# A decoder layer on one core: turnings grouped by bank, a tile in another pool, a scaling moved behind later splits

## The chip, the cores and the metric

The kernel runs on one core of a Trainium2 chip. The metric is the device time of one execution in microseconds (us). The kernel before takes 1844.71 us, the median of three runs (1843.94 to 1847.14).

## What is computed

One decoder layer on 256 tokens of width 2048, in float32:

```
x  = x + 0.5 * swiglu(rms_norm(x, ffn1_norm))             # D_FF = 5632
h  = rms_norm(x, mix_norm);  P = h @ w_in                  # columns split among head groups
     A: gated linear attention, 4 heads (dk 64, dv 128), output rms-normed per head and gated by silu(g_r)
     B: sparse attention, 8 query heads, 2 kv heads: compressed, selected and window branches
     C: cross-attention, 4 heads, into 256 memory tokens (memory normed, projected by w_mem_kv)
x  = x + concat(A, B, C) @ w_out
x  = x + 0.5 * swiglu(rms_norm(x, ffn2_norm))
y  = rms_norm(x, final_norm)
```

## The kernel before

**Products.** Every float32 product runs as three passes of TensorE. A chunk of weights, 128 x 1024 (512 KB), is loaded into a tile `r`; ScalarE copies it into a rounded tile `h` (L293), VectorE makes the remainder `l = r - h` (L294), and `mm3` (L313 to L316) issues left-high by `h`, left-low by `h` and left-high by `l`. In the trace these are the lines L314, L315 and L316, 128 x 512 each. `mmchunk` issues 12 of them for a chunk, and `product` eight chunks for a product. The left side of each product (`hh`/`hl`, `xh`/`xl`, `oh`/`ol`, `zh`/`zl`) is an activation that stands transposed in SBUF, also split in high and low.

**Stages.** `ffn1`, the mixing stage (projections "agq", "gkks", ..., "kwvs", "vw", the attention groups, then four products with `wout`) and `ffn2` follow each other. Each stage opens its own SBUF and PSUM pools (`stage`, L203) where the pools of the stage before lay, so a tile of a new stage may lie on bytes that an old tile held, and its first load then waits for the old tile's last reader.

**Turnings.** Between stages the residual `acc` is squared, turned by TensorE against an identity (`transposed`, L346, the turnings are L352), and split by ScalarE (L343) and VectorE (L344) with the gains of the next norm. One PSUM bank takes two blocks `k` of 128 columns, two turnings each. The last quarter of `acc` is turned inside the first product of the next stage (`turn_last`, L711).

**Norms.** `rstd` (L336) makes `(ss/n + eps)^-0.5` on GpSimd: a multiply-add (L338) and a power (L339). `headnorm` (L832) squares on VectorE (L834), sums (L835) and calls it.

**Order.** The program is written as one stream; a scheduler puts each engine's instructions into an order by the dependencies and the order of writing. `behind_products` (L297) pins what is written under it behind the latest split or product matmul of the engines named. `placed` calls a task ahead of a chunk of a product. All loads of weights go through SP's queue, in order, but for the adds of `ffn1u` and `ffn2u` from GpSimd, and for the first chunk of `ffn1g`, which ScalarE's queue issues.

**Around the change.** The gated output of group A stands in `ov` (L1040 to L1046): scaled by the head norm (L1045), multiplied by the gate (L1046), turned into `oh` by `turn_out` inside the projection "kwvs". The memory keys `mh` are scaled (L1218, L1219) and turned (L1226) inside the second memory product; the memory attention (scores L1259, softmax, turnings L1277, products L1289) is drained from there on. `gaT` is a small tile of the pool `own`, which lies below the pools `lo`, `raw` and `hi` of the mixing stage. Pool `ev` has two buffers of 128 x 512.

Of the kernel before, what the change touches and what calls it, by code (L numbers as in the profile page):

```python
# [22 lines left out]
D = 2048  # L23
# [168 lines left out]
def _body(tc, A):  # L192
# [24 lines left out]
    def bank():  # L217
        return psum("pm", "pm")
# [4 lines left out]
    def tbank():  # L223
        return psum("pt" if "pt" in P else "px", "pt")
# [76 lines left out]
            ex.enter_context(tc.issue_after(getattr(i, "ins", i)))  # L301
        return ex

    def chunk(src, parts=1, queue=nc.sync):
        n = src.shape[1]
        r = raw(n)
        for i in range(parts):
            sl = slice(i * n // parts, (i + 1) * n // parts)
            queue.dma_start(r[:, sl], src[:, sl])
        h, l = split(r, parts)  # L310
        return h.rearrange("p (k n) -> p k n", k=2), l.rearrange("p (k n) -> p k n", k=2)

# [10 lines left out]
            done["pe"] = mm3(banks[t][:, :n], ah[:, k0 + kk, sl], al[:, k0 + kk, sl], h[:, kk], l[:, kk],  # L323
                             first and kk == 0, last and kk == 1)

    def product(banks, ah, al, src, before=None, parts=1, queue=nc.sync):
        for c in range(8):
            if before:
                before(c)
            w = chunk(src[c], parts, queue) if c == 0 else chunk(src[c])  # L330
            mmchunk(banks, ah, al, 2 * c, w, c == 0, c == 7)

    def t16(name, dt=F32R):
# [1 line left out]

    def rstd(ss, inv_n, n, np_=128):  # L336
        y = small(n, "y")[:np_]
        pool.tensor_scalar(y, ss, inv_n, EPS, op0=ALU.mult, op1=ALU.add)  # L338
        pool.tensor_tensor(y, y, neghalf[:np_].to_broadcast([np_, n]), op=ALU.pow)  # L339
        return y  # L340

    def scaled_split(dh, dl, src, g):
        act.activation(dh, src, AF.Identity, scale=g)  # L343
        dve.scalar_tensor_tensor(dl, src, g, f(dh), op0=ALU.mult, op1=ALU.subtract)  # L344

    def transposed(j, g, th, tl, ks=range(4)):  # L346
        for k in ks:
            if k % 2 == 0:
                pt = (tbank() if "pt" in P else bank()).rearrange("p (k t) -> p k t", k=2)
            b = 4 * j + k  # L350
            for t in range(2):
                pe.transpose(pt[:, k % 2, t * 128:t * 128 + 128], acc[:, t, b * 128:b * 128 + 128], ident)  # L352
            scaled_split(th[:, b], tl[:, b], pt[:, k % 2], g[:, b:b + 1])

    def square_acc(ss, j):
        for t in range(2):
# [38 lines left out]
                 ("up", 5): lambda: put(3, 12, "tensor_add", 12, 22)}  # L395
        return (sh, sl), lambda *at: steps.get(at, lambda: None)()

    def ffn(name, th, tl, r, after, before=lambda i: None, by_rows=None, plain=(), queue=nc.sync):

# [23 lines left out]
        def first_slab():  # L425
            pg, pu = [bank(), bank()], [bank(), bank()]
            s4, made = combine(th, tl)

            def in_gate(c):
                before(c)  # L430
                made("gate", c)

            def in_up(c):
                made("up", c)
                before(("up", c))
                if c == 7:
                    for t in range(2):
                        st = t512("sil")
                        act.activation(st, pg[t], AF.Silu, scale=rr(t))
                        sil.append(st)  # L440

            sil, gs = [], []
            product(pg, th, tl, wg[0], in_gate, 2, queue)
            product(pu, th, tl, wu[0], in_up)
            for t in range(2):
                g = t512("g")
                dve.scalar_tensor_tensor(g, pu[t], rr(t), sil[t], op0=ALU.mult, op1=ALU.mult)
                gs.append(g)
            return s4, gs
# [144 lines left out]

    def load_x(c):
        r = t512("xT").rearrange("p (k t) -> p k t", k=2)
        nc.sync.dma_start(r, A["xT"][c])
        if c == 0:
            nc.sync.dma_start(gains, A["gains"])
        for k in range(2):  # L600
            b = 2 * c + k
            scaled_split(hh[:, b], hl[:, b], r[:, k], C["g1"][:, b:b + 1])
# [101 lines left out]
        elif at == (3, 10):  # L704
            norm_mem()

    ffn("ffn1", hh, hl, r1, after1, before1, queue=nc.scalar)
    xh, xl = st1["h"], st1["l"]
    r2, rm, r2q, r2n = (keep.tile([128, 2], F32, name=n) for n in ("r2", "rm", "r2q", "r2n"))

    def turn_last(c, ss, g, th, tl):  # L711

        if c == 1:

            for i in late_adds:
                tc.add_manual_dep(i.ins, done["dve"].ins.name, ORDER, reason="order")
        if c in (2, 3):
            with behind_products():
                transposed(3, g, th, tl, range(2 * c - 4, 2 * c - 2))
        if c == 4:  # L720
            with behind_products():
                square_acc(ss, 3)
# [72 lines left out]
    dve.tensor_scalar_add(gates, gates, 1.0)  # L795
    dve.reciprocal(gates, gates)

    gaT = own.tile([128, 256], F32, name="gaT")
    la = []

    def turn_ga():
# [227 lines left out]
        dve.tensor_tensor(sgr[:, t].rearrange("p (h d) -> p h d", h=4), xg.rearrange("p (h d) -> p h d", h=4),  # L1029
                          C["gon"].unsqueeze(1).to_broadcast([128, 4, 128]), op=ALU.mult)  # L1030

    ovs = []
    for t in range(2):
        pb = mbank()
        p3 = pb.rearrange("p (h d) -> p h d", h=4)
        for h in range(4):
            pe.matmul(p3[:, h], at[t][:, h], gv[:, t, h * 128:h * 128 + 128], start=True, stop=t == 0)
            if t == 1:
                pe.matmul(p3[:, h], at[2][:, h], gv[:, 0, h * 128:h * 128 + 128], start=False, stop=True)
        ov = t512("ov")  # L1040
        ovs.append(ov)
        act.activation(ov, pb, AF.Copy)
        rs = headnorm(ov, 4)
        o3 = ov.rearrange("p (h d) -> p h d", h=4)
        dve.tensor_tensor(o3, o3, rs.unsqueeze(2).to_broadcast([128, 4, 128]), op=ALU.mult)  # L1045
        dve.tensor_mul(ov, ov, sgr[:, t])  # L1046
    oh, ol = t16("oh"), t16("ol")

    def put_heads(src, k0, t):
# [11 lines left out]


    vsw = b4("vsw").rearrange("p (b c d) -> p b c d", b=2, c=2)
    b = proj("kwvs", both(spread("v", 0), placed((4, lambda: turn_out(0)), (5, lambda: turn_out(1)))))
    for t in range(2):
        s = r2[:, t:t + 1]
        v = ev("kw", 256)
# [167 lines left out]
    for i in range(2):  # L1235
        b = [bank(), bank()]
        for c in range(4):
            r = raw().rearrange("p (k t) -> p k t", k=4)
            nc.sync.dma_start(r, A["memT"][c])
            h = hi().rearrange("p (k t) -> p k t", k=4)  # L1240
            l = lo().rearrange("p (k t) -> p k t", k=4)
            for k in range(4):
                scaled_split(h[:, k], l[:, k], r[:, k], C["memg"][:, 4 * c + k:4 * c + k + 1])
            for e in range(2):
                if i == 1 and (c, e) == (1, 0):
                    with behind_products("pe"):
                        turn_mem()
                    for _ in mem_attention:
                        pass
                mmchunk(b, h, l, 2 * e, chunk(A["wmem"][i, 2 * c + e]), c == e == 0, c == 3 and e == 1)  # L1250
        if i == 0:
            mT.append(b4("mT").rearrange("p (h t) -> p h t", h=4))
            turn_mem = mem_heads(b, rm, C["mkn"], mT[1])
            pmT, bs, es = {}, {}, {}

            def scores(i):
                h, t = divmod(i, 2)
                bs[i] = mbank()[:, :256]
                pe.matmul(bs[i], mT[0][:, h, t * 128:t * 128 + 128], mT[1][:, h], start=True, stop=True)  # L1259

            def softmax(i):
                m, sums = small(1, "mm"), small(1, "ms")
                dve.tensor_reduce(m, bs[i], op=ALU.max, axis=AX.X)
                dve.tensor_scalar_mul(m, m, -SC)
                e = es[i] = t512("em")[:, :256]
                act.activation(e, bs[i], AF.Exp, bias=m, scale=SC, accum_out=sums)
                dve.reciprocal(sums, sums)
                dve.tensor_scalar_mul(e, e, sums)

            def apply(i):  # L1270
                h, t = divmod(i, 2)
                if i % 4 == 0:
                    pm2 = b4("pmT").rearrange("p (h c t) -> p h c t", h=2, c=2)
                    pmT[h], pmT[h + 1] = pm2[:, 0], pm2[:, 1]
                pt = tbank()
                for c in range(2):
                    pe.transpose(pt[:, c * 128:c * 128 + 128], es[i][:, c * 128:c * 128 + 128], ident)  # L1277
                act.activation(pmT[h][:, :, t * 128:t * 128 + 128],
                               pt[:, :256].rearrange("p (c t) -> p c t", c=2), AF.Copy)

            mem_attention = pipelined(8, scores, softmax, apply)
        else:
            mv = b4("mv").rearrange("p (t d) -> p t d", t=2)
            for t in range(2):
                scaled(mv[:, t], b[t], rm[:, t:t + 1])
# [52 lines left out]
    def finish(t, pd, s):  # L1338
# [6 lines left out]
            act.activation(junk, a, AF.Square, accum_out=ss3[:, t, 3 + i:4 + i])  # L1345
        s4 = small(1, "s4")
        dve.tensor_reduce(s4, ss3[:, t], op=ALU.add, axis=AX.X)
        dve.tensor_scalar(s4, s4, 1.0 / D, EPS, op0=ALU.mult, op1=ALU.add)
        r4 = small(1, "r4")
        pool.tensor_tensor(r4, s4, neghalf, op=ALU.pow)  # L1350
        dve.tensor_mul(acc[:, t, 1536:], acc[:, t, 1536:], gfin[0][:, 1536:])
        for j, queue in ((0, nc.sync), (3, nc.scalar), (1, nc.sync), (2, nc.scalar)):
            sl = slice(j * 512, j * 512 + 512)
# [22 lines left out]
```

## Time and profile before

| | us |
|---|---|
| median of three runs | 1844.71 |
| profiled execution, its own time | 1847.05 |
| its span in the trace | 1845.3 |
| PE busy in the span | 1820.4 |
| VectorE busy | 1637.9 |
| ScalarE busy | 1084.8 |
| GpSimd busy | 86.1 |

The span runs from the first to the last record of the one profiled execution; the execution's own time has 1.75 us around it. Idle time of PE is what can be gained without fewer matmuls, and each of its waits has a row that names the instruction it ended with.

### The profile page before, as it was taken

What the parts mean: (1) busy time and instruction counts of PE and PEld (TensorE: products, weight loads), DVE (VectorE), ACT (ScalarE), POOL (GpSimd) and SP (SyncE); (2) the same over time, 40 slices, a digit from 0 to 9 for tenths busy, and PEclk for the clock granted to TensorE, in tenths of its full rate; (3) what the DMA queues carried; (4) which work ended last, traced back from release to release, by engine and by line L of the source; (5) the groups of instructions that cost most, each with busy time, mean ns of one, the idle gap of its engine ahead of it and who ended that gap; (6) DMA issues with size and microseconds to landing.
All of it is one profiled execution on the core that took longest, in us unless ns stands there. A gap on an engine that the chain in (4) does not pass through costs nothing.

```text
span 1845.3 us, 23783 instructions
## 1 busy us (share of the span) xinstructions
PE 1820.4 (99%) x8465; PEld 1482.6 (80%) x8465; DVE 1637.9 (89%) x2107; ACT 1084.8 (59%) x1378; POOL 86.1 (5%) x107
## 2 busy tenths in 40 slices
PE   9999999999999999999999998999999999999997
PEld 7888888888888888777877786888888888888886
DVE  7999999999999988867677755899999999999996
ACT  7566666565656656534467644556656565666564
POOL 0000000000000000001000000000000000000000
PEclk9999999999999999999999999999999999999999
DMA  9877867776777636555634454776777677767771
GB/s 373 247 238 242 296 198 233 236 248 203 226 237 255 205 125 212 194 176 173 223 125 152 167 183 159 242 245 196 234 235 246 201 229 237 251 204 219 241 240 65
DMA packets 112231, 397.34 MB, mean 215 GB/s; under 512 B 12656, under 2 KB 12912, under 8 KB 111984
## 3 DMA queue, kind: packets, MB, share of 16 engines
q1 hardware_dynamic: 102608, 362.79, 56.3%
q0 software_dynamic: 8640, 31.46, 9.7%
q8 instruction: 66, 1.08, 0.2%
q10 hardware_dynamic: 864, 1.57, 0.2%
q14 instruction: 53, 0.43, 0.1%
HBM read 393.68 MB, written 2.10 MB: 214 GB/s over the span
## 4 chain that ended last, share of the span: by engine, by line
PE 91%; DVE 4%; DMA 2%; issue 1%; POOL 1%; ACT 1%; SPq 0%; POOLq 0%; DVEq 0%; ACTq 0%
PE pm L314 20%; PE pm L316 20%; PE pm L315 20%; PE px L314 9%; PE px L315 9%; PE px L316 9%; DVE l L294 1%; PE pt L409 1%; DMA r<-ffn1g 1%; PE px L932 1%; PE pm L969 0%; DMA r<-ffn1u 0%; PE po L1165 0%; DVE exg L1027 0%; POOL y L339 0%
## 5 line engine op out<-in xcount | busy, mean ns | idle before, releaser
L293 ACT ACTIVATE h<-r 128x1024 fp32r<-128x1024 f32 (+1 forms) x838 | 879.1, 1052 | 655.7 <-PE pm L316 456.8
L294 DVE TENSOR_TENSOR l<-r,h 128x1024 fp32r<-128x1024 f32 (+1 forms) x838 | 992.3, 1209 | 119.3 <-ACT h L293 107.2
L314 PE MATMUL px<-h,gx 128*128 128x512 f32 x616 | 239.7, 389 | 0.0
L315 PE MATMUL px<-l,gx 128*128 128x512 f32 x616 | 239.7, 389 | 0.0
L316 PE MATMUL px<-h,gx 128*128 128x512 f32 x616 | 239.6, 389 | 0.0
L314 PE MATMUL pm<-h,sh 128*128 128x512 f32 x480 | 189.2, 394 | 0.0
L315 PE MATMUL pm<-l,sh 128*128 128x512 f32 x480 | 188.5, 393 | 0.3 <-DVE l L294 0.3
L316 PE MATMUL pm<-h,sl 128*128 128x512 f32 x480 | 187.1, 390 | 0.0
L314 PE MATMUL pm<-h,zh 128*128 128x512 f32 x364 | 142.8, 392 | 0.9 <-ACT h L293 0.9
L315 PE MATMUL pm<-l,zh 128*128 128x512 f32 x364 | 142.5, 391 | 1.0 <-DVE l L294 1.0
L316 PE MATMUL pm<-h,zl 128*128 128x512 f32 x364 | 142.4, 391 | 0.0
L315 PE MATMUL pm<-l,hh 128*128 128x512 f32 x364 | 141.7, 390 | 0.5 <-DVE l L294 0.5
L314 PE MATMUL pm<-h,hh 128*128 128x512 f32 x364 | 141.4, 390 | 0.7 <-ACT h L293 0.5
L316 PE MATMUL pm<-h,hl 128*128 128x512 f32 x364 | 141.6, 389 | 0.0
L314 PEld LDWEIGHTS px<-h,gx 128*128 128x128 f32 x616 | 115.6, 188 | 24.2 <-DVE gx L412 0.2
L316 PEld LDWEIGHTS px<-h,gx 128*128 128x128 f32 x616 | 115.6, 188 | 24.0
L315 PEld LDWEIGHTS px<-l,gx 128*128 128x128 f32 x616 | 115.6, 188 | 24.0 <-DVE l L294 0.2
L314 PE MATMUL pm<-h,xh 128*128 128x512 f32 (+2 forms) x320 | 122.2, 382 | 0.9 <-ACT sq L358 0.9
L315 PE MATMUL pm<-l,xh 128*128 128x512 f32 (+2 forms) x320 | 120.4, 376 | 2.2 <-DVE l L294 2.2
L316 PE MATMUL pm<-h,xl 128*128 128x512 f32 (+2 forms) x320 | 121.1, 378 | 0.0
L423 DVE SCALAR_TENSOR_TENSOR acc<-px,acc 128x512 f32<-128x512 f32 x154 | 105.8, 687 | 6.0 <-PE px L316 5.9
L316 PEld LDWEIGHTS pm<-h,sl 128*128 128x128 f32 x480 | 90.2, 188 | 18.5
(343 smaller groups left out, 2640.1 us busy)
## 6 DMA issues: line engine op xcount, KB each, us to landing
r<-ffn1u SPq DMA_DIRECT2D x88, 512.0 KB, 5.1
r<-ffn1d SPq DMA_DIRECT2D x88, 512.0 KB, 4.9
r<-ffn2u SPq DMA_DIRECT2D x88, 512.0 KB, 5.1
r<-ffn2d SPq DMA_DIRECT2D x88, 512.0 KB, 4.8
r<-ffn1g SPq DMA_DIRECT2D x87, 512.0 KB, 5.2
r<-ffn2g SPq DMA_DIRECT2D x87, 512.0 KB, 5.3
r<-wout SPq DMA_DIRECT2D x32, 512.0 KB, 3.4
r<-ffn1u POOLq DMA_DIRECT2D x30, 512.0 KB, 7.2
```

What stands on the lines that cost most here:

```text
L293: done["act"] = act.activation(h[:, sl], r[:, sl], AF.Copy)
L294: done["dve"] = dve.tensor_sub(l[:, sl], r[:, sl], f(h[:, sl]))
L314: pe.matmul(out, ah, wh, start=first, stop=False)
L315: pe.matmul(out, ah, wl, start=False, stop=False)
L316: return pe.matmul(out, al, wh, start=False, stop=last)
L409: pe.transpose(pt[:, k], g[:, k * 128:k * 128 + 128], ident)
L423: return dve.scalar_tensor_tensor(a, pd, 0.5, a, op0=ALU.mult, op1=ALU.add)
L932: pe.matmul(pbs[h][:, li], lhs, rhs, start=True, stop=True)
```

## The change

- `transposed` issues all four turnings of a bank and only then the splits that read the bank; `turn_last` passes it the number of a bank instead of two blocks.
- `rstd` makes its multiply-add on VectorE, in place, and leaves only the power on GpSimd; the final norm (`finish`) uses it too, with the same instructions as before.
- The first loads: the gains and half of the first block of `x` go on ScalarE's queue, the other half of it and the first chunk of `ffn1g` on SP's.
- `gaT` moves from pool `own` to pool `ev`, so that `own` is 1024 bytes per partition smaller and `lo`, `raw` and `hi` lie lower.
- The two scalings of the gated output become `gla_scaled(t)`, called ahead of chunks 2 and 3 of "kwvs" behind the latest split on VectorE; `turn_out` moves from chunks 4 and 5 to 5 and 6.
- The memory keys are turned ahead of the product part (1, 1) instead of (1, 0), 12 matmuls later, and the memory attention with them.

```diff
-            queue.dma_start(r[:, sl], src[:, sl])
+            nc.sync.dma_start(r[:, sl], src[:, sl])
...
-        pool.tensor_scalar(y, ss, inv_n, EPS, op0=ALU.mult, op1=ALU.add)
-        pool.tensor_tensor(y, y, neghalf[:np_].to_broadcast([np_, n]), op=ALU.pow)
+        dve.tensor_scalar(ss, ss, inv_n, EPS, op0=ALU.mult, op1=ALU.add)
+        pool.tensor_tensor(y, ss, neghalf[:np_].to_broadcast([np_, n]), op=ALU.pow)
...
-    def transposed(j, g, th, tl, ks=range(4)):
-        for k in ks:
-            if k % 2 == 0:
-                pt = (tbank() if "pt" in P else bank()).rearrange("p (k t) -> p k t", k=2)
-            b = 4 * j + k
-            for t in range(2):
-                pe.transpose(pt[:, k % 2, t * 128:t * 128 + 128], acc[:, t, b * 128:b * 128 + 128], ident)
-            scaled_split(th[:, b], tl[:, b], pt[:, k % 2], g[:, b:b + 1])
+    def transposed(j, g, th, tl, pairs=range(2)):
+        for i in pairs:
+            pt = (tbank() if "pt" in P else bank()).rearrange("p (k t) -> p k t", k=2)
+            b = 4 * j + 2 * i
+            for k in range(2):
+                for t in range(2):
+                    pe.transpose(pt[:, k, t * 128:t * 128 + 128],
+                                 acc[:, t, (b + k) * 128:(b + k) * 128 + 128], ident)
+            for k in range(2):
+                scaled_split(th[:, b + k], tl[:, b + k], pt[:, k], g[:, b + k:b + k + 1])
...
         if c == 0:
-            nc.sync.dma_start(gains, A["gains"])
+            nc.scalar.dma_start(gains, A["gains"])
+            nc.sync.dma_start(r[:, 0], A["xT"][c][:, 0])
+            nc.scalar.dma_start(r[:, 1], A["xT"][c][:, 1])
...
-    gaT = own.tile([128, 256], F32, name="gaT")
+    gaT = ev("gaT", 256)
...
-        rs = headnorm(ov, 4)
+        rss.append(headnorm(ov, 4))
+
+    def gla_scaled(t):
+        ov = ovs[t]
         o3 = ov.rearrange("p (h d) -> p h d", h=4)
-        dve.tensor_tensor(o3, o3, rs.unsqueeze(2).to_broadcast([128, 4, 128]), op=ALU.mult)
+        dve.tensor_tensor(o3, o3, rss[t].unsqueeze(2).to_broadcast([128, 4, 128]), op=ALU.mult)
         dve.tensor_mul(ov, ov, sgr[:, t])
...
-    b = proj("kwvs", both(spread("v", 0), placed((4, lambda: turn_out(0)), (5, lambda: turn_out(1)))))
+    def scale_out(c):
+        if c in (2, 3):
+            with behind_products("dve"):
+                gla_scaled(c - 2)
+
+    b = proj("kwvs", both(spread("v", 0), scale_out, placed((5, lambda: turn_out(0)), (6, lambda: turn_out(1)))))
...
-                if i == 1 and (c, e) == (1, 0):
+                if i == 1 and (c, e) == (1, 1):
```

Three places in the engines' order show what moved.

TensorE, in the third and fourth chunk of the first gate product of `ffn2`, before (`acc` is the residual, `pm` a PSUM bank, `zh`/`zl` the product's left side):

```order
L352 MATMUL pm<-ident,acc 128x128 x2
L314 MATMUL pm<-h,zh 128x512
L315 MATMUL pm<-l,zh 128x512
L316 MATMUL pm<-h,zl 128x512
L314 MATMUL pm<-h,zh 128x512
L315 MATMUL pm<-l,zh 128x512
L316 MATMUL pm<-h,zl 128x512
L314 MATMUL pm<-h,zh 128x512
L315 MATMUL pm<-l,zh 128x512
L352 MATMUL pm<-ident,acc 128x128 x2
```

and with the change:

```order
L316 MATMUL pm<-h,zl 128x512
L352 MATMUL pm<-ident,acc 128x128 x4
L314 MATMUL pm<-h,zh 128x512
L315 MATMUL pm<-l,zh 128x512
L316 MATMUL pm<-h,zl 128x512
```

The second pair of turnings of the bank stood eight matmuls behind the first pair, behind the bank's first read; now the four stand together, and twelve matmuls follow.

VectorE, at the start of the projection "kwvs", before (`ov` is the gated output, `sqh` and `ssh` its head norm, `y` the power from GpSimd, `exc` of the compressed keys, `l` a split of weights):

```order
L834 TENSOR_TENSOR sqh<-ov 128x512
L1045 TENSOR_TENSOR ov<-ov,y 128x512
L835 TENSOR_REDUCE ssh<-sqh 128x4
L1046 TENSOR_TENSOR ov<-ov,sa 128x512
L1045 TENSOR_TENSOR ov<-ov,y 128x512
L988 TENSOR_SCALAR exc<-exc 128x64
L294 TENSOR_TENSOR l<-r,h 128x1024
L1046 TENSOR_TENSOR ov<-ov,sa 128x512
```

and with the change (L839 is the former L834, L840 L835, L1053 L1045, L1054 L1046):

```order
L839 TENSOR_TENSOR sqh<-ov 128x512
L338 TENSOR_SCALAR ssh<-ssh 128x4
L294 TENSOR_TENSOR l<-r,h 128x1024
L840 TENSOR_REDUCE ssh<-sqh 128x4
L993 TENSOR_SCALAR exc<-exc 128x64
L1053 TENSOR_TENSOR ov<-ov,y 128x512
L338 TENSOR_SCALAR ssh<-ssh 128x4
L994 RECIPROCAL exc<-exc 128x64
L1054 TENSOR_TENSOR ov<-ov,sa 128x512
```

The split `l` stood behind both scalings by `y`; now it stands ahead of both.

SP, at the first loads of `ffn2`, with what each waits for, before (the two of 128 x 512 are the halves of the first chunk):

```order
L309 DMA r<-ffn2g 128x512 [waits DMAHW5_49,DVE_49,PE_49]
L309 DMA r<-ffn2g 128x512
L309 DMA r<-ffn2g 128x1024 [waits DMAHW3_49,DVE_49,PE_49]
L309 DMA r<-ffn2g 128x1024 [waits DMAHW4_49]
L309 DMA r<-ffn2g 128x1024
```

and with the change:

```order
L309 DMA r<-ffn2g 128x512 [waits DMAHW6_49,DMAHW1_49,DVE_49]
L309 DMA r<-ffn2g 128x512
L309 DMA r<-ffn2g 128x1024 [waits DMAHW4_49,PE_49]
L309 DMA r<-ffn2g 128x1024 [waits DMAHW5_49,PE_49]
L309 DMA r<-ffn2g 128x1024
```

The first chunk's load no longer waits for TensorE; the second and the third do. By the tiles' addresses the old readers are: for the first the last split of `wout` on VectorE, for the second the end of the sixth `wout` chunk on TensorE, for the third TensorE's last `wout` matmul, for which the second waited before.

## Rows read from the trace of the kernel before

**Rows 1.** The page, part 1: busy us (share) xinstructions.

```profile
PE 1820.4 (99%) x8465; PEld 1482.6 (80%) x8465; DVE 1637.9 (89%) x2107; ACT 1084.8 (59%) x1378; POOL 86.1 (5%) x107
```

**Rows 2.** Waits of PE: us in total, times, longest us.

```profile
PE pm L315 <- DVE l L294: 4.0, 5, 2.2
PE pm L352 <- DVE zl L344: 3.5, 1, 3.5
...
PE pt L1160 <- DVE e L1149: 0.9, 1, 0.9
PE pt L1226 <- DVE mh L1219: 0.9, 1, 0.9
...
PE pt L352 <- DVE xl L344: 0.7, 1, 0.7
```

**Rows 3.** Timeline of PE in "kwvs": start us, us, instruction [idle before <-releaser].

```profile
846.38 0.64 PE L969 MATMUL pm<-r,flat 128*32 128x256 f32 x8
849.19 0.79 PE L315 MATMUL pm<-l,xh 128*128 128x512 f32 x1 [2.17 <-DVE l L294]
...
852.62 0.40 PE L315 MATMUL pm<-l,xh 128*128 128x512 f32 x1
```

**Rows 4.** Windows: busy us of each engine, granted PE clock, DMA share, GB/s.

```profile
850.00:855.00 5.00, 5.00 (x19) 3.59 (x18) 4.31 (x9) 1.19 (x3) 0.00 (x0) 0.76 0.72 219
1150.00:1155.00 5.00, 3.21 (x12) 2.58 (x13) 5.00 (x9) 3.69 (x6) 1.81 (x2) 0.78 0.82 306
...
1040.00:1045.00 5.00, 5.00 (x26) 3.79 (x24) 4.62 (x14) 3.85 (x12) 0.00 (x0) 1.00 0.82 283
```

**Rows 5.** Timeline of VectorE (DVE) in "kwvs".

```profile
844.14 0.69 DVE L1045 TENSOR_TENSOR ov<-ov,y 128x512 f32<-128x512 f32 x1 [1.18 <-POOL y L339]
...
847.21 0.69 DVE L1045 TENSOR_TENSOR ov<-ov,y 128x512 f32<-128x512 f32 x1 [1.18 <-POOL y L339]
...
847.92 1.22 DVE L294 TENSOR_TENSOR l<-r,h 128x1024 fp32r<-128x1024 f32 x1
```

**Rows 6.** Timeline of PE in the first gate product of `ffn2`.

```profile
1147.87 0.39 PE L315 MATMUL pm<-l,zh 128*128 128x512 f32 x1
1151.79 0.44 PE L352 MATMUL pm<-ident,acc 128*128 128x128 f32 x2 [3.53 <-DVE zl L344]
...
1152.77 0.60 PE L316 MATMUL pm<-h,zl 128*128 128x512 f32 x1
...
1156.41 0.40 PE L315 MATMUL pm<-l,zh 128*128 128x512 f32 x1
```

**Rows 7.** Timeline of PE at the change from `wout` to `ffn2`.

```profile
1134.12 0.39 PE L315 MATMUL pm<-l,oh 128*128 128x512 f32 x1
...
1137.07 0.39 PE L316 MATMUL pm<-h,ol 128*128 128x512 f32 x1
...
1143.39 0.50 PE L315 MATMUL pm<-l,zh 128*128 128x512 f32 x1 [0.76 <-DVE l L294]
```

**Rows 8.** Waits of SP's DMA queue from 1100 to 1146 us.

```profile
SPq L309 <- PE pm L315: 10.9, 1, 10.9
SPq L309 <- PE pm L316: 2.0, 1, 2.0
```

**Rows 9.** Timeline of ScalarE (ACT) in the first gate product of `ffn2`.

```profile
1141.02 1.06 ACT L293 ACTIVATE h<-r 128x1024 fp32r<-128x1024 f32 x1 [2.31 <-DMA r<-ffn2g]
```

**Rows 10.** Timeline of PE at the start of the program.

```profile
9.30 0.73 PE L314 MATMUL pm<-h,hh 128*128 128x512 f32 x2 [0.46 <-ACT h L293]
10.56 0.50 PE L315 MATMUL pm<-l,hh 128*128 128x512 f32 x1 [0.53 <-DVE l L294]
```

**Rows 11.** DMA busy share in tenths, 0 to 12 us in 40 slices.

```profile
DMA  0000004669999999997888899999899999999999
```

**Rows 12.** Groups by line: busy us, mean ns | idle before.

```profile
L338 POOL TENSOR_SCALAR y<-ssh 128x4 f32<-128x4 f32 (+2 forms) x15 | 9.1, 605 | 297.8 <-DVE ssh L835 297.8
L1132 DVE TENSOR_SCALAR nm<-m 128x2 f32<-128x2 f32 x16 | 2.6, 165 | 0.1
```

More of the change, by code (lines that the diff above doesn't have):

```diff
@@ L302, in behind_products, with chunk @@
         return ex
-    def chunk(src, parts=1, queue=nc.sync):
+    def chunk(src, parts=1):
         n = src.shape[1]
@@ L324, in mmchunk, with product @@
                              first and kk == 0, last and kk == 1)
-    def product(banks, ah, al, src, before=None, parts=1, queue=nc.sync):
+    def product(banks, ah, al, src, before=None, parts=1):
         for c in range(8):
@@ L329, in product @@
                 before(c)
-            w = chunk(src[c], parts, queue) if c == 0 else chunk(src[c])
+            w = chunk(src[c], parts if c == 0 else 1)
             mmchunk(banks, ah, al, 2 * c, w, c == 0, c == 7)
@@ L396, in combine, with ffn @@
         return (sh, sl), lambda *at: steps.get(at, lambda: None)()
-    def ffn(name, th, tl, r, after, before=lambda i: None, by_rows=None, plain=(), queue=nc.sync):
+    def ffn(name, th, tl, r, after, before=lambda i: None, by_rows=None, plain=()):
         wg, wu, wd = A[name + "g"], A[name + "u"], A[name + "d"]
@@ L442, in first_slab @@
             sil, gs = [], []
-            product(pg, th, tl, wg[0], in_gate, 2, queue)
+            product(pg, th, tl, wg[0], in_gate, 2)
             product(pu, th, tl, wu[0], in_up)
@@ L596, in load_x @@
         r = t512("xT").rearrange("p (k t) -> p k t", k=2)
-        nc.sync.dma_start(r, A["xT"][c])
         if c == 0:
-            nc.sync.dma_start(gains, A["gains"])
+            nc.scalar.dma_start(gains, A["gains"])
+            nc.sync.dma_start(r[:, 0], A["xT"][c][:, 0])
+            nc.scalar.dma_start(r[:, 1], A["xT"][c][:, 1])
+        else:
+            nc.sync.dma_start(r, A["xT"][c])
         for k in range(2):
@@ L705, in before1 @@
             norm_mem()
-    ffn("ffn1", hh, hl, r1, after1, before1, queue=nc.scalar)
+    ffn("ffn1", hh, hl, r1, after1, before1)
     xh, xl = st1["h"], st1["l"]
@@ L718, in turn_last @@
             with behind_products():
-                transposed(3, g, th, tl, range(2 * c - 4, 2 * c - 2))
+                transposed(3, g, th, tl, (c - 2,))
         if c == 4:
@@ L1030, in _body @@
                           C["gon"].unsqueeze(1).to_broadcast([128, 4, 128]), op=ALU.mult)
-    ovs = []
+    ovs, rss = [], []
     for t in range(2):
@@ L1347, in finish @@
         dve.tensor_reduce(s4, ss3[:, t], op=ALU.add, axis=AX.X)
-        dve.tensor_scalar(s4, s4, 1.0 / D, EPS, op0=ALU.mult, op1=ALU.add)
-        r4 = small(1, "r4")
-        pool.tensor_tensor(r4, s4, neghalf, op=ALU.pow)
+        r4 = rstd(s4, 1.0 / D, 1)
         dve.tensor_mul(acc[:, t, 1536:], acc[:, t, 1536:], gfin[0][:, 1536:])
```

## The prediction

> **What bounds the kernel now.** The page's first part [rows 1] says that PE is busy 1820.4 of the span's 1845.3 us. No edit takes a product matmul away, so what can be won is PE's waiting and whatever makes its matmuls slower. The view to read next is therefore the list of what PE waited for [rows 2]. Two entries stand out by their longest wait: 2.2 us for a split `l`, and 3.5 us for `zl`, the split of a turned block. I looked both up in PE's timeline. The first [rows 3] is in "kwvs", the second [rows 6] in the first product of `ffn2`.
>
> Both are followed by slow matmuls. In steady work 13 matmuls take 1137.07 - 1134.12 = 2.95 us [rows 7], 0.227 us each. Behind the first wait, from 849.19 to 852.62 [rows 3], eight take 3.43 us, 0.43 each. The windows there have a mean granted clock of 0.76 and 0.78 [rows 4], so part of each ran at the lower of the two levels, 1.2 instead of 2.4 GHz. PE had done nothing for 2.2 and 3.5 us just before. So each of these waits costs more than its length: 3.43 - 8 x 0.227 = 1.6 us on top in "kwvs"; in `ffn2` 3.64 us from 1152.77 to 1156.41 [rows 6] hold eight matmuls and a pair of turnings (0.2 us), again 1.6 us too much.
>
> **The change part by part.** Gains are counted in PE's time, since PE waits for the others here.
>
> Turnings by bank. In `ffn2`, L352 came 3.92 us behind the matmul ahead of it [rows 6], 3.7 more than a step. It waited for VectorE's `zl` of the bank's first half, since the second pair goes into the same bank. VectorE was busy 5.00 of 5.00 us in that window [rows 4] and came late. With the four turnings together nothing on PE waits for that read; `zl` of these blocks is next needed by the product's seventh chunk. The read had eight matmuls of time (1.8 us) before the second pair and came 3.7 us late; from the third chunk to the seventh it has some 4 x 12 x 0.227 = 10.9 us. Gain 3.7 + 1.6 = **5.3 us**. The same wait exists once for `xl` in the first mixing product, 0.7 us [rows 2]: gain **0.7**. The first read of a bank starts two turnings later, about 0.15 us; nothing waits for it that closely, so it costs nothing.
>
> Scaling behind the later splits. In "kwvs" VectorE twice stood idle for 1.18 us for the power from GpSimd, with the split `l` queued behind; it began at 847.92 [rows 5], and PE's L315 at 849.19. In the new order the split follows the second `sqh`, which ended before 844.14 - 1.18 = 842.96 [rows 5]. It is then done at about 842.96 + 0.15 + 1.22 = 844.3, and PE wants it at 847.0 (846.38 + 0.64). The moved work, some six operations of at most 0.6 us from one start to the next and several of 0.1, then delays the next split to about 848.8, wanted 12 matmuls after the first, at 849.8. One microsecond to spare is little, yet enough. Gain 2.2 + 1.6 = **3.8 us**. Late next: `ov` itself, which only the turnings read, and these moved a chunk (2.7 us) back. The new order of the attention groups behind it is bounded with the small waits below.
>
> `gaT`. The pools of the mixing stage move down by 1024 bytes and no longer lie on the first tile `r` of `ffn2`. SP's queue stood 10.9 us for a matmul L315 and then 2.0 us for the last L316 of `wout` [rows 8], so the two first chunks of `ffn2` came late. PE took 6.32 us from 1137.07 to 1143.39 [rows 7] for 14 steps, 3.2 us at the usual pace: 3.1 us lost. Now the first chunk is loaded while `wout` still runs, the second from the end of its sixth chunk, 24 matmuls or 5.4 us earlier. The third now waits for the last matmul, as the second did. That one was issued at about 1137.5, and its copy could start at 1141.02 [rows 9]. With a copy of 1.06 and a split of 1.22 us, the third is whole at about 1143.3; PE wants its `l` at 1137.3 + 24 x 0.227 + 0.2 = 1142.95. So some 0.35 us come back: gain **2.8 us**. In `ev` the tile rotates among two buffers, and the tiles around it have had their last reader chunks before; no load and no split is behind it. Price nothing, at most one wait of 0.9 (the size in [rows 2]).
>
> Memory keys. The turning waited 0.9 us for `mh` [rows 2]. Twelve matmuls later is 2.7 us: gain **0.9**. What it costs is a memory attention that falls into the first `wout` product, between fewer matmuls (a rival below).
>
> Multiply-add on VectorE. It leaves GpSimd's 605 ns and comes to VectorE at 165 ns for an operation of that size [rows 12]. There are 19, 3.1 us in all, none of them in a stretch where PE waits for VectorE but those counted above. Where VectorE waits for the power (1.18 us, rows 5's case) it saves some 0.4. Together with the new order it moves a split of 1.22 us ahead of the scaled `e` in the window attention, so that the wait of 0.9 for `e` [rows 2] turns into one of about the same size for that split: I count **0.5**, between -0.3 and 1.2.
>
> First loads. PE waits 0.46 and 0.53 us for the second chunk [rows 10]. The bytes that are loaded ahead of that chunk are the same as before, and the DMA engines are 0.9 and more busy from about 3 us on [rows 11]. PE may begin half a microsecond earlier and then waits the same longer for that chunk. I take **0**, between -0.5 and 1.0 (both waits gone). The Trainium skill ("DMA: Bandwidth & Descriptors", "Issuing engines are not separate DMA queues") says that transfers started by several engines share the same DMA engines, so that a second queue saves only the time of starting them. By that rule the term is near nothing; by the first matmul's start alone it would be up to 0.5 us; rows 11 side with the rule.
>
> Sum: 5.3 + 0.7 + 3.8 + 2.8 + 0.9 + 0.5 = 14.0 us. Against it I set new small waits of a reordered program, one of the usual 0.9 us and a few tenths: 1.2 us (0 to 4). Net 12.8 us. The profiled execution took 1847.05 us and would take 1834.2. It lies 2.3 us above the median of the runs, to which the forecast is referred: 1844.71 - 12.8 = **1832 us**.
>
> **The rivals.**
>
> 1. One long wait comes back. VectorE is full at both places; if its work ahead of the next split takes a microsecond longer than I added up, PE stands again, and above some 2 us the slow stretch follows. With "kwvs" unmended the gain is 9.0 and the time 1835.7; with `ffn2` unmended 7.5 and 1837.2. For it: the spare microsecond in "kwvs". Against: the deadline in `ffn2` moved back by 9 us.
>
> 2. VectorE sets the end of both stretches, so that both long waits only shift. The change then is worth what `gaT`, the keys and the small terms bring: 2.8 + 0.9 + 0.7 + 0.5 - 1.2 = 3.7 us, 1841.0. For it: VectorE's 5.00 of 5.00 [rows 4]. Against: it stood idle for 2 x 1.18 us in "kwvs" [rows 5] and could not split `ffn2`'s first chunk while SP held its load back for 10.9 us [rows 8]; the edits let it use both.
>
> 3. Slower: memory attention inside `wout`. The list of PE's instructions has 12 product matmuls among its eight pairs of turnings where there were 20. If each step then waits for its softmax on VectorE and ScalarE, PE may fall to the lower clock, as behind the two long waits, and stay there. At that level a matmul costs 0.2 us more [rows 3], so it outweighs the sum and makes the kernel slower by over 3.7 us from (12.8 + 3.7) / 0.2 = 82 matmuls on; a `wout` product has 96. All of them: 1832 + 19 = 1851. Against: in 1040 to 1045 the same chain ran with a granted clock of 1.00 [rows 4], and the waits of 0.9 us in rows 2 were in windows without a slow matmul.
>
> 4. More: the small waits cost nothing, the first loads save their 1.0: 1829.8 and less.
>
> **How the numbers follow.** My case 0.62, rival 1 0.22, rival 2 0.08, rival 3 0.05, rival 4 0.03. What a measurement here can tell from no change is about 0.2%, 3.7 us, so faster means below 1841.0. My case, rivals 1 and 4 lie there, and a little of rival 2: faster 0.88; the rest of rival 2 is the same, 0.07; slower 0.05. The range takes in my case with its bounds (1828 to 1835) and rival 1 with 2 us for the spread of the runs: 1828 to 1839.
>
> **What would show it.** Right: no L352 among PE's waits with over 0.5 us, and no L315 with over 1 us outside the window attention; windows of a granted clock of 1.00 throughout; the first `ffn2` chunk's copy long before the last `wout` matmul, and some 3.6 us instead of 6.32 over the steps of rows 7; the keys' turnings without a wait; the start within 0.5 us. Wrong: a window under 0.9 anywhere, or a new wait of over 1 us in "kwvs", in the attention groups or in `wout`.

## The result and the profile after

| | before | with the change |
|---|---|---|
| median of six runs, us | 1846.11 | 1835.1 |
| lowest to highest | 1843.94 to 1850.02 | 1834.57 to 1836.3 |
| span of the profiled execution | 1845.3 | 1834.5 |

The ratio of the runs is 0.994 with a 95% interval from 0.9927 to 0.9952. Three more runs of the kernel before moved its own median from 1844.71 to 1846.11, so the gain is 11.0 us where 12.8 were forecast. The forecast time was 1832; the forecast gain from the new median would give 1833.3.

PE's waits in the profile of the change (us in total, times, longest us) answer to [rows 2]:

```profile
PE pm L315 <- DVE l L294: 2.0, 3, 1.0
PE po L283 <- DVE warm L280: 1.2, 1, 1.2
PE pt L1240 <- DVE mh L1233: 0.9, 1, 0.9
PE pm L314 <- ACT sq L360: 0.9, 1, 0.9
...
PE pm L352 <- DVE acc L425: 0.3, 1, 0.3
```

The 2.2 us for a split, the 3.5 us for `zl` and the 0.7 us for `xl` are gone. The wait for `mh` (now L1240) is as long as it was. The clock answers to [rows 4]; the windows are those of "kwvs", of the memory attention and of the first product of `ffn2` (busy us of PE, PEld, DVE, ACT, POOL, then granted PE clock, DMA share, GB/s):

```profile
850.00:855.00 5.00, 5.00 (x29) 3.90 (x26) 4.44 (x8) 1.97 (x6) 2.24 (x1) 1.00 0.72 220
...
1035.00:1040.00 5.00, 5.00 (x24) 3.87 (x22) 4.10 (x10) 3.16 (x7) 0.00 (x0) 1.00 0.80 256
...
1140.00:1145.00 5.00, 5.00 (x27) 3.87 (x26) 5.00 (x5) 4.97 (x8) 0.00 (x0) 1.00 1.03 419
1145.00:1150.00 5.00, 5.00 (x24) 4.13 (x23) 4.81 (x10) 2.43 (x5) 1.60 (x1) 1.00 1.02 389
```

All stand at 1.00, the memory attention's too. At the change to `ffn2`, PE's timeline now reads

```profile
1134.64 0.39 PE L316 MATMUL pm<-h,ol 128*128 128x512 f32 x1
...
1137.82 0.39 PE L315 MATMUL pm<-l,zh 128*128 128x512 f32 x1
...
1140.32 0.60 PE L352 MATMUL pm<-ident,acc 128*128 128x128 f32 x4
...
1143.82 0.60 PE L352 MATMUL pm<-ident,acc 128*128 128x128 f32 x4
```

The fourteen steps that took 6.32 us [rows 7] take 1137.82 - 1134.64 = 3.18, and no turning waits. ScalarE's copies of the first three chunks:

```profile
1126.53 1.28 ACT L293 ACTIVATE h<-r 128x512 fp32r<-128x512 f32 x2 [3.95 <-DMA r<-ffn2g]
1133.45 1.06 ACT L293 ACTIVATE h<-r 128x1024 fp32r<-128x1024 f32 x1 [5.64 <-DMA r<-ffn2g]
1138.77 1.06 ACT L293 ACTIVATE h<-r 128x1024 fp32r<-128x1024 f32 x1 [4.26 <-DMA r<-ffn2g]
```

The first two are done before `wout` ends.

To see where the time went I set the start of each of the 7512 product matmuls (L314 to L316) beside the start of the one with the same number in the other trace. The difference changes for good where one kernel waits, or runs at the lower clock, and the other does not; smaller steps, where the two have other work between the same matmuls, come back soon after. It ends at -10.8 us:

| place | forecast | traces, before to after |
|---|---|---|
| start and first products, to 64 us | 0 | +0.4 |
| `xl` in the first mixing product | -0.7 | -1.1, then +0.4 for another wait; -0.3 net from 64 to 760 us |
| "kwvs" | -3.8 | -3.7 |
| compressed keys and queries, 880 to 940 us | part of +1.2 | +1.5 |
| window attention | -0.5 | -0.35 |
| memory keys and memory attention | -0.9 | +0.2 |
| change to `ffn2` and turnings there | -2.8 and -5.3 | -8.4 |

### The profile page after: what moved, and what is told of

Its sections match the earlier page's. It is cut to its first block, busy times and chain, and to the rows that moved or that the text cites. A ratio compares the mean times of both kernels' runs of the same rounds, so it can differ in the third digit from the quotient of the medians.

```text
span 1834.5 us, 23779 instructions
## 1 busy us (share of the span) xinstructions
PE 1816.5 (99%) x8465; PEld 1482.4 (81%) x8465; DVE 1639.7 (89%) x2126; ACT 1086.5 (59%) x1378; POOL 82.6 (5%) x88
## 3 DMA queue, kind: packets, MB, share of 16 engines
q10 hardware_dynamic: 864, 1.21, 0.2%
## 4 chain that ended last, share of the span: by engine, by line
PE 92%; DVE 3%; DMA 2%; ACT 1%; issue 1%; POOL 0%; SPq 0%; POOLq 0%; DVEq 0%; ACTq 0%
PE pm L314 20%; PE pm L316 20%; PE pm L315 20%; PE px L314 9%; PE px L316 9%; PE px L315 9%; DVE l L294 1%; PE pt L411 1%; DMA r<-ffn1u 1%; DMA r<-ffn1g 1%; PE po L1179 1%; PE pm L974 1%; PE px L937 1%; ACT h L293 0%; POOL y L339 0%
## 5 line engine op out<-in xcount | busy, mean ns | idle before, releaser
L314 PE MATMUL px<-h,gx 128*128 128x512 f32 x616 | 239.8, 389 | 0.0
L316 PE MATMUL px<-h,gx 128*128 128x512 f32 x616 | 239.7, 389 | 0.0
L314 PE MATMUL pm<-h,sh 128*128 128x512 f32 x480 | 189.1, 394 | 0.0
L316 PE MATMUL pm<-h,sl 128*128 128x512 f32 x480 | 187.2, 390 | 0.0
L314 PE MATMUL pm<-h,hh 128*128 128x512 f32 x364 | 142.1, 392 | 0.5 <-ACT h L293 0.5
L314 PE MATMUL pm<-h,zh 128*128 128x512 f32 x364 | 141.9, 390 | 0.0
L316 PE MATMUL pm<-h,zl 128*128 128x512 f32 x364 | 141.7, 389 | 0.0
L316 PE MATMUL pm<-h,hl 128*128 128x512 f32 x364 | 141.6, 389 | 0.0
L314 PEld LDWEIGHTS px<-h,gx 128*128 128x128 f32 x616 | 115.7, 188 | 24.3 <-DVE gx L414 0.3
L316 PEld LDWEIGHTS px<-h,gx 128*128 128x128 f32 x616 | 115.7, 188 | 24.1
L314 PE MATMUL pm<-h,xh 128*128 128x512 f32 (+2 forms) x320 | 122.8, 384 | 1.1 <-ACT sq L360 0.9
L316 PE MATMUL pm<-h,xl 128*128 128x512 f32 (+2 forms) x320 | 120.1, 375 | 0.0
L316 PEld LDWEIGHTS pm<-h,sl 128*128 128x128 f32 x480 | 90.2, 188 | 18.5
```

Of the source, the lines that this page charges most:

```text
L314: pe.matmul(out, ah, wh, start=first, stop=False)
L316: return pe.matmul(out, al, wh, start=False, stop=last)
```

## The experiments

Each differs from the change by the edit shown, or from the kernel before where that is said. The change ran again beside three of them (u_rstd, b_rstd, b_turn). Differences below are against that run (1834.38 us), or by numbered matmuls against its trace, or for the two "b_" runs against the kernel before. The other runs were on two other chips, where the kernel before had medians of 1847.79 us (u_turn, u_scale, u_gat, u_loads) and 1847.89 (u_keys, keys_end, best, dose) and not 1846.42. Their differences in time are therefore uncertain by some 1.4 us, and the ratio to the kernel before on the same chip stands beside them.

**after_again.** No edit.

> The change itself once more, beside the next kernels on their chip: 1834.5 to 1836 us. If the waits of 0.4 to 0.6 us near 718, 881, 906 and 930 us in its first trace belong to the program, they stand here too; if they are chance of one execution, some are gone.

Measured: 1834.38 us (1833.58 to 1835.28), ratio to before 0.9939 (0.9925 to 0.9952), a little under the expected times. Of the 1.5 us lost between 880 and 940 us, 0.35 + 0.39 + 0.40 are gone in this trace: most of that row is the chance of one execution. The wait near 718 us stands here too (0.4).

**u_turn.** Each block turned and read in turn.

> The change without its turnings by bank (each block is turned and read before the next block of its bank is turned, as before). Theory A, each part has its own wait: PE's wait for zl in the first product of ffn2 and the slow stretch behind it come back, 3.7 + 1.6 us, and 0.7 us for xl: 1835.1 + 6 = 1841 us. Theory B, the wait for zl was only a consequence of the late first chunks of ffn2, which gaT's move mends: L352 waits under 1 us there, the clock stays whole, and the time is 1835 to 1836.5 us.

```diff
-            for k in range(2):
                 scaled_split(th[:, b + k], tl[:, b + k], pt[:, k], g[:, b + k:b + k + 1])
```

Measured: 1842.75 us, 8.4 more; ratio 0.9975 (0.9966 to 0.9985), by which it would be 6.6. Its waits and a window:

```profile
PE pm L352 <- DVE zl L344: 4.5, 1, 4.5
...
PE pt L352 <- DVE xl L344: 1.6, 1, 1.6
```

```profile
1145.00:1150.00 5.00, 1.99 (x7) 1.69 (x8) 4.81 (x10) 2.15 (x4) 1.60 (x1) 0.80 1.03 402
```

Both waits and the slow stretch are back, 6.35 us by the numbered matmuls in `ffn2`. Theory B falls: with the first chunks in time the wait for `zl` is not shorter but longer, 4.5 us where it was 3.5, since PE comes earlier to the turning.

**b_turn.** The kernel before with the turnings of the change.

> The kernel before with the turnings by bank alone. Theory A: the wait of 3.5 us for zl with its slow stretch and the 0.7 us for xl are gone, the late first chunks of ffn2 stay: 6 us faster, ratio 0.9967. Rival: VectorE, late by those chunks, holds PE up at the next splits instead, 2.5 us of it come back: 3.5 us faster, ratio 0.9981.

Measured: 1841.26 us, ratio 0.9977 (0.9967 to 0.9987), 5.2 us less than the kernel before on the same chip. In `ffn2` the matmuls gain 5.3 us, as theory A has it, and the window has a full clock:

```profile
1145.00:1150.00 5.00, 5.00 (x28) 4.15 (x27) 5.00 (x7) 5.00 (x9) 0.20 (x1) 1.00 1.03 418
```

At `xl` they gain 1.1 us, of which 0.9 return, mostly in a wait of 0.6 for a copy on ScalarE. The time is between the two theories.

**u_gat.** `gaT` in its old pool.

> The change with gaT back in its old pool. Theory A: the first two chunks of ffn2 are late again, PE loses 2.1 to 2.8 us there and nothing else moves, since no turning waits for VectorE any more: 1837.5 us. Theory B: VectorE, behind by the late chunks, holds PE up once more in the product that follows, by 3 us or more: 1841 us.

```diff
-    gaT = ev("gaT", 256)
+    gaT = own.tile([128, 256], F32, name="gaT")
```

Measured: 1839.03 us, 4.7 more; ratio 0.9957 (0.9945 to 0.997), by which it would be 3.3. PE's timeline and the windows:

```profile
1139.65 0.50 PE L314 MATMUL pm<-h,zh 128*128 128x512 f32 x1 [0.95 <-ACT h L293]
1140.91 0.50 PE L315 MATMUL pm<-l,zh 128*128 128x512 f32 x1 [0.76 <-DVE l L294]
```

```profile
1135.00:1140.00 5.00, 3.68 (x13) 2.34 (x13) 2.91 (x5) 1.78 (x3) 0.00 (x0) 1.00 0.80 271
1140.00:1145.00 5.00, 4.24 (x14) 3.15 (x14) 4.51 (x5) 4.32 (x8) 0.00 (x0) 0.71 1.01 401
```

The fourteen steps of [rows 7] take 6.51 us again where the change has 3.18, so the late chunks cost 3.3. But the clock then fell to its lower level, and that is the rest of the 4.9 us at this place. It is not theory B: no turning and no later split waits. In the kernel before, where the waits for the second chunk were 0.53 and 0.76 us, the clock did not fall there.

**u_scale.** The two scalings at once, the turnings ahead of chunks 4 and 5.

> The change with the gated output scaled at once, as before, and turned ahead of chunks 4 and 5. Theory A: the split for the second half of kwvs' chunk stands behind two waits for GpSimd again, PE waits about 2.2 us there and eight slow matmuls follow: 1835.1 + 3.7 = 1838.8 us. Rival: with the multiply-add on VectorE the two waits are 0.4 us shorter each, PE's wait is then about 1.4 us, no slow matmuls follow, 1836.5 us.

```diff
-        rss.append(headnorm(ov, 4))
...
+        rs = headnorm(ov, 4)
         o3 = ov.rearrange("p (h d) -> p h d", h=4)
-        dve.tensor_tensor(o3, o3, rss[t].unsqueeze(2).to_broadcast([128, 4, 128]), op=ALU.mult)
+        dve.tensor_tensor(o3, o3, rs.unsqueeze(2).to_broadcast([128, 4, 128]), op=ALU.mult)
...
-    b = proj("kwvs", both(spread("v", 0), scale_out, placed((5, lambda: turn_out(0)), (6, lambda: turn_out(1)))))
+    b = proj("kwvs", both(spread("v", 0), placed((4, lambda: turn_out(0)), (5, lambda: turn_out(1)))))
```

Measured: 1836.22 us, 1.8 more, but with the ratio of the change (0.994): the difference in time is not shown. By the matmuls at this place it is 1.3. VectorE and PE there:

```profile
842.33 1.22 DVE L294 TENSOR_TENSOR l<-r,h 128x1024 fp32r<-128x1024 f32 x1
844.44 0.70 DVE L1050 TENSOR_TENSOR ov<-ov,y 128x512 f32<-128x512 f32 x1 [0.90 <-POOL y L339]
```

```profile
850.52 0.60 PE L1000 MATMUL px<-kept,hT 128*32 128x128 f32 x4 [1.19 <-DVE hT L995]
```

The split goes ahead of the scaling although the scaling is written first. No wait for it is left; 1.2 us for `hT`, of the compressed keys, stand in its place, and the window from 850 us has a clock of 1.00. Theory A falls; the rival's time came, but what PE waits for is another tile.

**u_rstd.** The multiply-add of the norms on GpSimd.

> The change with the multiply-add of the norms back on GpSimd. Its VectorE order in kwvs has the split behind both scalings again, although they are written behind later splits. Theory C, the multiply-add's move put the split ahead and the scaling's move did not: PE waits for that split by 2.2 us or more, slow matmuls follow, 1839 to 1840 us. Theory A, the scaling's move did it: no such wait, and the chains of the norms are longer by some 0.4 us where they count, 1835 to 1836 us.

```diff
-        dve.tensor_scalar(ss, ss, inv_n, EPS, op0=ALU.mult, op1=ALU.add)
-        pool.tensor_tensor(y, ss, neghalf[:np_].to_broadcast([np_, n]), op=ALU.pow)
+        pool.tensor_scalar(y, ss, inv_n, EPS, op0=ALU.mult, op1=ALU.add)
+        pool.tensor_tensor(y, y, neghalf[:np_].to_broadcast([np_, n]), op=ALU.pow)
```

Measured: 1836.82 us, 2.4 more; 1.9 by the matmuls at this place. PE there:

```profile
848.37 0.27 PE L1000 MATMUL px<-kept,hT 128*32 128x128 f32 x1 [1.28 <-DVE hT L995]
...
850.01 0.50 PE L315 MATMUL pm<-l,xh 128*128 128x512 f32 x1 [0.57 <-DVE l L294]
```

The split is behind both scalings, as theory C said, but it came at 848.74 us and PE had other work until then: the wait is 0.57, not 2.2, and the slow stretch stays away. Neither theory is right alone.

**b_rstd.** The kernel before with that multiply-add on VectorE.

> The kernel before with the multiply-add on VectorE alone. Theory C: the wait of 2.2 us in kwvs and its slow matmuls are gone, at most a wait of 1.2 us for the compressed keys in their place: 2.6 to 3.8 us faster than before, ratio 0.9980 to 0.9986. Theory A: no faster than before by more than 0.5 us.

Measured: 1844.69 us (11 runs), ratio 0.9991 (0.9982 to 1.0). VectorE at "kwvs":

```profile
843.50 1.22 DVE L294 TENSOR_TENSOR l<-r,h 128x1024 fp32r<-128x1024 f32 x1
845.62 0.69 DVE L1045 TENSOR_TENSOR ov<-ov,y 128x512 f32<-128x512 f32 x1 [0.90 <-POOL y L339]
```

The split stands ahead of the scaling, the matmuls there gain 2.5 us, as theory C has it, and a wait of 1.2 for `hT` is left. In `ffn2` the clock fell already at the late chunks, as in u_gat:

```profile
1140.00:1145.00 5.00, 3.88 (x9) 2.90 (x10) 4.20 (x4) 4.14 (x8) 0.00 (x0) 0.68 1.01 406
```

PE came later to the turning, waited 1.6 us for `zl` instead of 3.5, and no slow stretch followed that wait. By the end the gain is 3.5 us in the trace, 1.7 between the medians, and the interval reaches 1.0: what the edit is worth by itself in time stays open.

**u_loads.** The first loads as before.

> The change with the first loads as before (first weights on ScalarE's queue, x and gains on SP's). In the trace of the change PE's first matmul is 0.74 us earlier than before, its work at 30 us is 0.92 us later and at 58 us 0.28 us later. Theory A, these loads are worth nothing or cost a little: 1834.2 to 1835.1 us, and PE's work at 30 us stands 0.9 us earlier than in the change. Rival, they are worth the earlier start: 1835.8 us.

```diff
+        nc.sync.dma_start(r, A["xT"][c])
         if c == 0:
-            nc.scalar.dma_start(gains, A["gains"])
-            nc.sync.dma_start(r[:, 0], A["xT"][c][:, 0])
-            nc.scalar.dma_start(r[:, 1], A["xT"][c][:, 1])
...
+            nc.sync.dma_start(gains, A["gains"])
...
-    ffn("ffn1", hh, hl, r1, after1, before1)
+    ffn("ffn1", hh, hl, r1, after1, before1, queue=nc.scalar)
```

Measured: 1834.34 us, the same as the change; ratio 0.9929 (0.9916 to 0.9941), whose interval overlaps that of the change. In the trace the 97th matmul starts at 29.64 us, in the change at 30.32 and 31.0. Over all traces: with the old loads (five kernels) the 25th starts between 12.83 and 13.25 us, with the new ones (nine traces) between 13.18 and 15.03, although their first matmul is 0.5 to 0.8 us earlier. Theory A holds. The three latest of the nine, 14.8 to 15.0 us, are u_keys, keys_end and dose. There PE waited 1.1 to 1.3 us and then 0.5 for the second chunk, and the clock fell to its lower level behind that, as in u_keys:

```profile
10.00:15.00 5.00, 4.47 (x13) 3.19 (x12) 5.00 (x8) 4.70 (x9) 0.00 (x0) 0.66 1.04 409
```

In the other six the 25th starts by 13.88. None of the five traces with the old loads has such a stretch. That the new loads bring it is not shown by so few.

**u_keys.** The memory keys ahead of part (1, 0) again.

> The change with the memory keys turned ahead of product part (1, 0) again. The order of TensorE's instructions, by kind and tile, is the same as in the change, so the move of the line should be worth nothing: PE waits 0.9 us for mh as in the change. Rival, which the forecast held: without the move 0.9 us are lost.

```diff
-                if i == 1 and (c, e) == (1, 1):
+                if i == 1 and (c, e) == (1, 0):
```

Measured: 1834.4 us in one run, and PE waits 0.9 us for `mh`, as in the change. The move of the line did nothing: PE's matmuls stand in the same order with it and without it. The turnings do stand six and ten product matmuls later than in the kernel before; b_rstd has them there too and u_rstd has not, so it was the multiply-add that moved them.

**keys_end.** The bound moved behind the whole product.

> The change with the memory keys turned, and the memory attention run, behind the last chunk of the second memory product, so that the turnings really stand later in TensorE's order. Theory: the wait of 0.9 us for mh goes and nothing takes its place: 0.9 us faster than the change, 1833.5 us. Rival: the attention then waits for its softmax between fewer matmuls of wout, 1 us or more comes back there: 1834.5 to 1836 us.

```diff
-                if i == 1 and (c, e) == (1, 1):
-                    with behind_products("pe"):
-                        turn_mem()
-                    for _ in mem_attention:
-                        pass
...
             for t in range(2):
                 scaled(mv[:, t], b[t], rm[:, t:t + 1])
+            with behind_products("pe"):
+                turn_mem()
+            for _ in mem_attention:
+                pass
```

Measured: 1833.61 us, ratio to before 0.9924 (0.9911 to 0.9938). The turnings:

```profile
1032.87 0.60 PE L1240 MATMUL pt<-ident,mh 128*128 128x128 f32 x4
1033.70 0.63 PE L1240 MATMUL pt<-ident,mh 128*128 128x128 f32 x4 [0.23 <-DVE mh L1233]
```

By the matmuls 0.8 us are gained from there to the end of the attention. The median agrees (on the same chip u_keys, with PE's order of the change, took 1834.4), but the interval overlaps that of the change: faster in the trace, not shown in the time.

**best.** keys_end with the old loads.

> keys_end and the first loads as before together: if both edits are worth what their traces say (0.9 and 0.9 us), 1832.6 us; if neither is, 1834.5 us.

Measured: 1834.21 us, 0.9927 (0.9915 to 0.994). That is near the second of the two times: the gains of the traces don't add up in the time, where the runs of one kernel spread by 1 to 2 us.

**dose.** Extra powers on GpSimd.

> The change with 25 extra powers on GpSimd, of the 128 x 4 size of a head norm, on a constant tile, spread over the fifth slab of ffn1, where VectorE runs splits and adds that read two tiles in SBUF. Theory, a power waits for the VectorE operation that runs when it starts: those that start alone take 1.0 us, the others up to 1.2 us more, by what is left of that operation. Rival, the long powers in the change were long for another reason: all 25 take about 1.0 us. Nothing waits for them, so the time stays.

```diff
+    dosed = const.tile([128, 4], F32, name="dosed")
+    pool.memset(dosed, 2.0)
...
+        elif at[0] == 4:
+            pool.tensor_tensor(small(4, "y"), dosed, neghalf.to_broadcast([128, 4]), op=ALU.pow)
```

Measured: 1835.48 us. The scheduler put all 25 at the program's start, back to back from 0.95 us, not into the fifth slab. That serves as well: VectorE's first operation on two tiles in SBUF starts at 4.74 us. The group by line, up to 4.6 us and from 16 to 37 us (busy us, mean ns | idle before):

```profile
L712 POOL TENSOR_TENSOR y<-dosed,neghalf 128x4 f32<-128x4 f32 x4 | 3.9, 1004 | 0.1
...
L712 POOL TENSOR_TENSOR y<-dosed,neghalf 128x4 f32<-128x4 f32 x13 | 21.2, 1655 | 0.0
```

Alone a power takes 1.00 us; beside VectorE's splits and adds 1.66 in the mean. Up to 1.2 more was expected; the longest, 2.82 us, is 1.8 more. It let two operations of VectorE pass, the one that ran and the next:

```profile
20.61 2.82 POOL L712 TENSOR_TENSOR y<-dosed,neghalf 128x4 f32<-128x4 f32 x1
```

```profile
20.47 0.96 DVE L385 TENSOR_TENSOR r<-hh,hl 128x768 f32<-128x768 f32 x1
21.34 1.22 DVE L296 TENSOR_TENSOR l<-r,h 128x1024 fp32r<-128x1024 f32 x1
```

It ended at 23.43, 0.87 us behind the end of the second (22.56). All 16 powers that took over 1.1 us ended 0.86 to 0.87 us behind the end of a VectorE operation with two inputs in SBUF. The other nine, of 1.00 to 1.02 us, began when none ran, or in the last 0.06 us of one. Five of these nine ran after 6 us, beside work of TensorE and ScalarE, so it is not theirs that stretches a power.

## Why the prediction was right, and where its steps were wrong

The gain came out 2 us under the forecast in the trace. The memory keys (0.9 forecast) gave nothing, the `xl` term (0.7) 0.3 net, and the first loads and the new waits cost 0.4 and 0.3 more than was set down.

**Turnings by bank** (5.3 + 0.7) and **gaT** (2.8): right in place, mechanism and sum for `ffn2`: 8.4 us against 8.1. u_turn and b_turn show the wait and the slow stretch with the one part missing or alone. For `gaT` the price was right in the change (6.32 to 3.18 us over the fourteen steps); without it u_gat lost 3.3 over these steps and, with the clock's fall, 4.9. The clock fell there in b_rstd too, and not in the kernel before and in b_turn. Rival 1's "above some 2 us the slow stretch follows" was read from two waits and is not the whole rule.

**Scaling behind the later splits** (3.8): the size was right (3.7), the cause was not. The step "in the new order the split follows the second `sqh`" gave the whole gain to the moved scaling. u_scale shows that the split goes there without that edit, b_rstd that the multiply-add's move is enough for it. Why the scheduler then puts the split first is not shown. Each edit alone leaves 1.2 to 1.3 us for `hT`; together they leave nothing. Over the same 90 matmuls PE takes 27.2 us before, 24.8 with the multiply-add alone (b_rstd), 25.4 with the scaling and no multiply-add there (u_rstd) and 23.5 with both. The order showed all edits at once, and I read it as the effect of one; that the size fits is owed to this order and not to the reason given.

**Memory keys** (0.9): wrong. "Twelve matmuls later is 2.7 us" took the line for the place in the order; u_keys shows that the line moves nothing, and keys_end what a binding move does (0.8 us in the trace). There is a second part to it. In the change GpSimd's power for the keys reads, on GpSimd and VectorE,

```profile
1029.34 1.82 POOL L339 TENSOR_TENSOR y<-ssh,neghalf 128x4 f32<-128x4 f32 x1 [2.92 <-DVE ssh L338]
```

```profile
1029.08 1.22 DVE L294 TENSOR_TENSOR l<-r,h 128x1024 fp32r<-128x1024 f32 x1
...
1031.19 0.69 DVE L1232 TENSOR_TENSOR mh<-mh,y 128x512 f32<-128x512 f32 x1 [0.90 <-POOL y L339]
```

and in the kernel before

```profile
1030.17 1.01 POOL L339 TENSOR_TENSOR y<-y,neghalf 128x4 f32<-128x4 f32 x1
```

The power ran beside a split and took 0.8 us more; it ended 0.86 us behind the end of that split (1030.30), as the powers of the dose did.

**Multiply-add on VectorE** (0.5): the sum held in the window attention (0.35). The saving of "some 0.4" per norm did not: in "kwvs" VectorE's wait for the power fell from 1.18 to 0.90 us (u_scale, b_rstd), and for the keys PE's wait stayed. There are two reasons. The 605 ns was a mean that held waits of GpSimd for VectorE. In the kernel before, a multiply-add of this size took 1.02 us at 1026.00, beside a split, and where VectorE did nothing when it began,

```profile
975.63 0.19 POOL L338 TENSOR_SCALAR y<-ssh 128x4 f32<-128x4 f32 x1 [42.04 <-DVE ssh L835]
```

which is hardly more than VectorE's 0.165. And the split that VectorE runs next now stretches the power. The larger part of what this edit gave, the place of the split in "kwvs", was in no term of it.

**First loads** (0, between -0.5 and 1.0): a loss of 0.4 us by 64 us. The later chunk, not the first matmul, decides, as was argued; that PE waits longer for it with the new loads was not. The Trainium skill says that starting transfers from several engines saves only the time of starting them ("DMA: Bandwidth & Descriptors", "Issuing engines are not separate DMA queues"). The traces agree: the first matmul starts at 5.08 us instead of 5.82, and the DMA engines moved 290 GB/s over the first 12 us of its trace where it was 312.

**New small waits** (1.2): 1.5 us between 880 and 940 us in the first trace, 0.3 in the second.

**Rivals.** One long wait coming back and VectorE as the bound: no; its window from 1140 us is full in the change too (5.00 of 5.00) and PE waits for nothing there. Memory attention at the lower clock: no, 1.00. Of the signs that were named, the keys' wait did not go; and a window under 0.9 stands at the start of u_keys, which has PE's order of the change, though not in the two traces of the change itself.

## What to carry to other kernels

A wait is worth its length plus the slow matmuls behind it; look for both, and expect that the clock's part can return at another place where waits are left. Where a scheduler sets the order, test each line of a change against the order by itself: most of the gain in "kwvs" came from an edit that was not written for it, and one edit moved nothing. A short operation taken off GpSimd shortens a chain only if the engine that takes it doesn't run, right behind, what GpSimd must wait for. Take the price of an operation from one that ran alone, not from a mean that may hold waits.

## What was not expected of the hardware

A GpSimd power that starts while VectorE runs an operation on two SBUF tiles waits for its end, and sometimes for the next one's too: 1.00 us alone, up to 2.82 us beside such work. The Trainium skill names the contention ("SBUF — State Buffer", "Who interferes with whom": a VectorE instruction with two SBUF inputs contends with a GpSimd instruction that reads SBUF). The dose agrees, with ends 0.86 to 0.87 us behind those of VectorE's operations. The other way round no wait is seen there: splits that began while a power ran, at 6.57 and 9.76 us, took 0.69 and 1.23 us as usual.

The clock fell to its lower level without a long wait: in u_gat behind four waits of 0.35, 0.23, 0.95 and 0.76 us (the window of 0.71 above) and in b_rstd behind 0.43, 0.23, 1.00 and 0.76 (0.68). In the kernel before 0.37, 0.23, 0.53 and 0.76 left it whole, in b_turn 0.53, 0.22, 0.67 and 0.76. At the program's start 1.13 and 0.53 lowered it in keys_end, and 1.21 and 0.53 left it whole in after_again. What decides between them no run here shows.
